# Two plain tiles instead of four at three feed-forward entries of a decoder trunk

## The chip, the core and the metric

The kernel runs on one core of a Trainium2 chip. The metric is device time in microseconds (us) of one execution. Five engines of the core matter here: TensorE (PE in the profile; its weight loads are PEld), VectorE (DVE), ScalarE (ACT), GpSimd (POOL) and SyncE (SP). SP and POOL are here mostly queues that issue transfers (DMAs). Each engine works through its own instructions in order, and waits on semaphores for the others.

## What is computed

The reference is a decoder trunk of two layers on 512 tokens with 1024 features, all in float32. Each layer is

```
x = x + 0.5 * swiglu(rms_norm(x, ffn1_norm[l]), ffn1_w_in[l], ffn1_w_out[l])
h = rms_norm(x, mix_norm[l]) @ w_mix_in[l]
...                                   # three token mixers on h give y
x = x + y @ w_mix_out[l]
x = x + 0.5 * swiglu(rms_norm(x, ffn2_norm[l]), ffn2_w_in[l], ffn2_w_out[l])
```

with `rms_norm(x, g) = x * rsqrt(mean(x*x) + 1e-6) * g` and `swiglu(h, w_in, w_out) = (silu(gate) * up) @ w_out`, where `gate` and `up` are the two halves of `h @ w_in`. A feed-forward block (FFN) has 2816 hidden features, 22 tiles of 128. There are four FFNs: two in each layer.

## The kernel before

**Layout.** The residual stream lies transposed in `xT`: 8 tiles of 128 features by 512 tokens. A float32 product is made from three matmuls on parts: a high part (rounded to the type that TensorE reads at full rate) and a low part (the remainder) of each operand, and high*high, high*low, low*high are summed (`mm3`, lines 328, 336 and 337). So every weight block is first parted: ScalarE casts the high part (line 314 for plain work, line 810 for the other kind), VectorE subtracts it from the weights for the low part (lines 315 and 812). The two parts lie in a tile `hl`, of which there are three in turn.

**Two ways for the first FFN product.** A pair of hidden tiles (256 gate and 256 up features) can be made *plain*: for each of the 8 feature tiles of x, 4 output banks times 3 matmuls of 512 tokens, 96 matmuls. The plain way takes x times the norm's gain, without the factor 1/rms; the factor `inv` is multiplied onto the result afterwards (`clear`, `values`). Or it can be made in *halves*: a scheme with 7 products, P1 to P7 in the order `ORDER_IN` = P1, P2, P6, P5, P7, P3, P4, in place of 8 (Strassen's, in Winograd's form). Each product is 8 blocks times 3 matmuls of 256 tokens, 24 in all. The halves way needs sums of quarters of the *normalised* x (`xn`, parted into `xc`), and sums of quarters of the weights (`raw`, `sums`), so it can't begin before the norm's factor is known.

**An entry.** Where an FFN begins, the norm's factor isn't known yet: x has just been finished. So the first tiles are made plain, and meanwhile the squares are summed (`sqa`), averaged over the features by two matmuls with a matrix of 1/1024 (line 447), and turned into `inv`: on ScalarE Ln, Exp and Square (line 277) and a load of the table for Silu (line 268), on VectorE three steps (lines 431 to 433). `covered` is the number of plain tiles: 6 in the first FFN of the kernel (`cover`), and 4 in the other three (`enter`, lines 583 to 699). Those three are the second FFN of layer 0, the first FFN of layer 1 and the second FFN of layer 1. In the profile their plain work begins at 578.11, 902.70 and 1467.33 us. `enter` writes out by hand the order of the entry on ScalarE and VectorE: `follow` chains each instruction behind the one before it on its engine. After `inv`, VectorE makes the quarters of normalised x, `xn`, each by four operations of 256 tokens (line 619); ScalarE casts their sums to high parts (line 632), VectorE makes the low parts (635 and 637) and the sums (642).

**The planner.** `plan(covered)` lists the products of the halves way in order, and at which step each load, sum and part of weights is issued. The weight parts of a product are made three products ahead (`prepare`, lines 800 to 812). For the first halved pair, `halved` loads four weight quarters (line 863), adds one quarter onto another by a transfer that accumulates (line 786, on POOL), and `enter` prepares the weights of the first products itself. A second accumulating transfer (line 827) adds a tile from on-chip memory onto another.

**Before the entry.** The last four feature tiles of x are finished by a loop on VectorE: in the mixer's end the add of line 1230, in an FFN's end the scaled add of line 502. After each, `norm_part` makes x times gain as high and low part (lines 408 and 409) and the square and its sum (lines 424 and 425).

Of the kernel before, what the change touches and what calls it, by code (L numbers as in the profile page):

```python
# [24 lines left out]
P = 128  # L25
T = 512
# [14 lines left out]
FIRST = 6  # L41
# [118 lines left out]
class Trunk:  # L160
# [255 lines left out]

    def squared(self, j, xj, pool):
# [25 lines left out]

    def end_norm(self, bank, pool, parts, keep=False):
        nc = self.nc
        for n, part in enumerate(parts):
            nc.tensor.matmul(bank, self.ones_mean, part, start=n == 0, stop=n == 1)
# [10 lines left out]
    def ffn(self, w_in, w_out, next_gain, covered, begin=None, out=None):  # L458
        nc = self.nc
        tc = self.tc  # L460
        with tc.tile_pool(name=self.n("ffn"), bufs=1) as fp:
# [26 lines left out]
            for dg in range(2):  # L488
# [10 lines left out]
                for i in range(4):  # L499
                    j = dg * 4 + i  # L500
                    xj = self.xT[:, j, :]
                    nc.vector.scalar_tensor_tensor(
                        out=xj, in0=banks[i], scalar=0.5, in1=xj,
                        op0=ALU.mult, op1=ALU.add,
                    )
                    if next_gain is not None:
                        self.norm_part(j, fp)
# [75 lines left out]
    def enter(self, fp, w_in, then):  # L583
        nc = self.nc
        H = T // 2
        A, V = (lambda i, e=e: self.follow(e, i) for e in "av")

        def stream(f, banks, given):
            def parts(k, kk):
                r = slice(k * P, (k + kk) * P)  # L590
                return [w_in[r, f * P : (f + 2) * P], w_in[r, FF + f * P : FF + (f + 2) * P]]

            return self.stream_steps(
                [(bk, slice(c, c + P), None) for bk, c in zip(banks, (0, 256, 128, 384))],
                parts, self.xact, KD, given=given,
            )

        ba = self.next4()
        first = stream(0, ba, lambda k: k == KD - 2)
        for _ in range(4):  # L600
            next(first)
        parts = self.parted_norm(fp, ("g1", "g1"), 2, True)
        nb = self.bank("pt" if self.ntog % 2 == 0 else "po")
        bb = self.next4()
        second = stream(2, bb, lambda k: True)
        self.ngain = self.const.tile([P, KD], F32, tag="ngain", name=self.n("ngain"))
        A(nc.scalar.activation(self.ngain, self.gain, AF.Copy, scale=-1.0))
        next(second)
        self.end_norm(nb, fp, parts, True)
        self.table(SILU)  # L610
        next(first, None)
        next(then)
        X, self.xc, lows = {}, {}, {}

        def quarter(a, b):
            X[a, b] = t = fp.tile([P, 4, H], F32, tag=f"r{2 + 2 * a + b}", name=self.n("xn"))
            for k in range(4):
                i = 4 * a + k
                V(nc.vector.scalar_tensor_tensor(
                    out=t[:, k, :], in0=self.xT[:, i, b * H : (b + 1) * H],  # L620
                    scalar=(self.gain if a == b else self.ngain)[:, i : i + 1],
                    in1=self.inv[:, b * H : (b + 1) * H], op0=ALU.mult, op1=ALU.mult,
                ))

# [19 lines left out]
        def both(name):  # L644
            high(name)
            lows[name]()

        def row():
            next(second)
            next(second, None)  # L650

        cleared = {}

        def clear(f, i):
            banks = bb if f else ba
            cleared[f, i] = self.clear(fp, banks[2 * i], banks[2 * i + 1], True)

        def values(f, i):
            self.values(fp, f, i, *cleared.pop((f, i)), True)

# [4 lines left out]
        next(second)  # L665
        next(second)
        high("P2")
        quarter(0, 1)
# [1254 lines left out]
```

## Time and profile before

| | us |
|---|---|
| median of 3 runs | 1802.08 (1801.78 to 1804.31) |
| the profiled execution | 1801.38 |
| its span, from first to last instruction | 1799.6 |
| TensorE busy | 1792.0 |
| VectorE busy | 1430.1 |
| ScalarE busy | 1001.0 |
| POOL busy | 176.6 |

The page gives busy times, the chain of work that ended last, and the costliest groups of instructions by line. A row such as `L810 ACT CAST hl<-w 128x1024 ... x322 | 336.8, 1050 | 305.9 ...` reads: line 810, on ScalarE, a cast that writes the tile `hl` from `w`, 322 times, 336.8 us in all, 1050 ns each, with 305.9 us of idle time ahead of them. A row of the timeline gives start, length, engine, line, operation, tiles and shape; `x4` says that four such instructions were merged into one row. Instructions of one engine overlap a little, so the distance between two starts is shorter than a length. TensorE's rows overlap strongly, and for it only the distance between starts is used.

### The profile page before, as it was taken

What the parts mean: (1) busy time and instruction counts of PE and PEld (TensorE: products, weight loads), DVE (VectorE), ACT (ScalarE), POOL (GpSimd) and SP (SyncE); (2) the same over time, 40 slices, a digit from 0 to 9 for tenths busy, and PEclk for the clock granted to TensorE, in tenths of its full rate; (3) what the DMA queues carried; (4) which work ended last, traced back from release to release, by engine and by line L of the source; (5) the groups of instructions that cost most, each with busy time, mean ns of one, the idle gap of its engine ahead of it and who ended that gap; (6) DMA issues with size and microseconds to landing.
All of it is one profiled execution on the core that took longest, in us unless ns stands there. A gap on an engine that the chain in (4) does not pass through costs nothing.

```text
span 1799.6 us, 34747 instructions
## 1 busy us (share of the span) xinstructions
PE 1792.0 (100%) x14271; PEld 1681.0 (93%) x14271; DVE 1430.1 (79%) x2006; ACT 1001.0 (56%) x1445; POOL 176.6 (10%) x184
## 2 busy tenths in 40 slices
PE   9999999999999999999999999999999999999999
PEld 7899999899888899999889999998998888999997
DVE  9889787676888798879679887876868879888793
ACT  5455554464776465556446555555547755555551
POOL 0011120100000002112001111201000000020210
PEclk9999999999999999999999999999999999999999
DMA  7659793233433857868265786913334346597762
GB/s 207 180 133 196 169 188 97 71 82 84 106 98 108 222 130 170 194 163 166 82 207 133 169 185 175 187 65 83 78 85 116 89 144 179 141 185 190 160 133 94
DMA packets 244638, 254.09 MB, mean 141 GB/s; under 512 B 18904, under 2 KB 228576, under 8 KB 244480
## 3 DMA queue, kind: packets, MB, share of 16 engines
q1 hardware_dynamic: 189424, 182.38, 33.7%
q0 software_dynamic: 54752, 69.23, 23.8%
q8 instruction: 112, 1.84, 0.4%
q14 instruction: 46, 0.38, 0.1%
q10 hardware_dynamic: 304, 0.27, 0.0%
HBM read 223.98 MB, written 2.10 MB: 126 GB/s over the span
## 4 chain that ended last, share of the span: by engine, by line
PE 94%; DVE 2%; ACT 2%; DMA 1%; issue 1%; SPq 0%; POOL 0%; ACTq 0%; DVEq 0%; POOLq 0%
PE mm L328 14%; PE mm L336 14%; PE mm L337 14%; PE sc L328 6%; PE sc L336 6%; PE sc L337 6%; PE pt L336 6%; PE pt L328 6%; PE pt L337 6%; PE po L328 4%; PE po L336 4%; PE po L337 4%; PE po L1654 1%; PE pt L1698 1%; PE pt L1352 1%
## 5 line engine op out<-in xcount | busy, mean ns | idle before, releaser
L810 ACT CAST hl<-w 128x1024 fp32r<-128x1024 f32 x322 | 336.8, 1050 | 305.9 <-PE mm L337 80.4
L812 DVE TENSOR_TENSOR hl<-w,hl 128x1024 fp32r<-128x1024 f32 x322 | 391.8, 1220 | 96.7 <-ACT hl L810 96.7
L315 DVE TENSOR_TENSOR hl<-st,hl 128x512 fp32r<-128x512 f32 (+3 forms) x196 | 162.5, 830 | 116.2 <-ACT hl L314 115.0
L314 ACT CAST hl<-st 128x512 fp32r<-128x512 f32 (+3 forms) x196 | 143.1, 732 | 174.3 <-PE po L337 66.8
L328 PE MATMUL mm<-xc,hl 128*128 128x256 f32 (+1 forms) x733 | 201.3, 276 | 0.0
L336 PE MATMUL mm<-xc,hl 128*128 128x256 f32 x728 | 201.2, 276 | 0.0
L337 PE MATMUL mm<-xc,hl 128*128 128x256 f32 x728 | 201.0, 276 | 0.0
L328 PE MATMUL sc<-xc,hl 128*128 128x256 f32 (+1 forms) x532 | 146.0, 276 | 0.0
L336 PE MATMUL sc<-xc,hl 128*128 128x256 f32 x528 | 146.0, 276 | 0.0
L337 PE MATMUL sc<-xc,hl 128*128 128x256 f32 x528 | 145.8, 276 | 0.0
L328 PEld LDWEIGHTS mm<-xc,hl 128*128 128x128 f32 x733 | 137.4, 188 | 0.2
L337 PEld LDWEIGHTS mm<-xc,hl 128*128 128x128 f32 x728 | 136.7, 188 | 0.0
L336 PEld LDWEIGHTS mm<-xc,hl 128*128 128x128 f32 x728 | 136.7, 188 | 0.0
L328 PE MATMUL pt<-xc,hl 128*128 128x256 f32 (+1 forms) x482 | 132.6, 276 | 0.0
L336 PE MATMUL pt<-xc,hl 128*128 128x256 f32 x480 | 132.6, 276 | 0.0
L337 PE MATMUL pt<-xc,hl 128*128 128x256 f32 x480 | 132.5, 276 | 0.0
L328 PE MATMUL mm<-x,hl 128*128 128x512 f32 x272 | 107.6, 396 | 0.0
L336 PE MATMUL mm<-x,hl 128*128 128x512 f32 x272 | 106.3, 391 | 0.0
L337 PE MATMUL mm<-x,hl 128*128 128x512 f32 x272 | 106.2, 390 | 0.0
L328 PEld LDWEIGHTS sc<-xc,hl 128*128 128x128 f32 x532 | 99.7, 188 | 0.2
L336 PEld LDWEIGHTS sc<-xc,hl 128*128 128x128 f32 x528 | 99.1, 188 | 0.0
L337 PEld LDWEIGHTS sc<-xc,hl 128*128 128x128 f32 x528 | 99.1, 188 | 0.0
(517 smaller groups left out, 5575.0 us busy)
## 6 DMA issues: line engine op xcount, KB each, us to landing
w<-in_ffn_w_in_dram SPq DMA_DIRECT2D x140, 512.0 KB, 5.1
w<-in_ffn_w_out_dram SPq DMA_DIRECT2D x64, 512.0 KB, 5.2
w<-in_ffn_w_out_dram POOLq DMA_DIRECT2D x56, 512.0 KB, 7.2
st<-in_w_mix_in_dram SPq DMA_DIRECT2D x88, 256.0 KB, 2.8
st<-in_ffn_w_in_dram SPq DMA_DIRECT2D x70, 256.0 KB, 3.1
w<-in_ffn_w_in_dram POOLq DMA_DIRECT2D x35, 512.0 KB, 8.9
w<-S POOLq DMA_DIRECT2D x35, 512.0 KB, 4.7
st<-in_ffn_w_out_dram SPq DMA_DIRECT2D x24, 512.0 KB, 5.3
```

What stands on the lines that cost most here:

```text
L314: a = nc.scalar.copy(hi, src[:, c : c + w])
L315: b = nc.vector.tensor_sub(lo, src[:, c : c + w], hi)
L328: i = nc.tensor.matmul(acc[:, c], ah, bh[:, c], start=first and c.start == 0, stop=False, skip_group_check=True,)
L336: nc.tensor.matmul(acc, a, b, start=False, stop=False, skip_group_check=True)
L337: i = nc.tensor.matmul(acc, c, d, start=False, stop=last, skip_group_check=True)
L810: A(nc.scalar.copy(hi, src))
L812: return lambda: V(nc.vector.tensor_sub(lo, src, hi))
L1352: nc.tensor.matmul(bank[hh][rows[par], at + x * n : at + (x + 1) * n], held[rows[hh], c * CH : (c + 1) * CH], moving(rows[hh], c), start=T ...
L1654: nc.tensor.matmul(self.ob[:, t0 + u * P : t0 + 2 * P], V[:, j, h % 4].rearrange("p a d -> p (a d)"), part[:, j, u:, :].rearrange("p i t - ...
L1698: nc.tensor.transpose(tb[:, j * P : (j + 1) * P], p[:, j * P : (j + 1) * P], self.ident)
```

## The change

At the three entries two tiles are made plain, not four; the second pair goes the halves way. The work around it is written out anew:

- In the loops that finish the last four x tiles ahead of a changed entry, the squares and their sums come first, right behind each add (`norm_late`). The parts of x times gain for these four tiles (`scaled`) move into the entry, two tiles at a time.
- The averaging matmuls (`mean`) are issued apart from the rest of the norm (`factor`).
- The quarters of normalised x are made in two steps: ScalarE scales x by the gain (`grown`, before `inv` is needed), and VectorE multiplies a whole quarter by `inv` in one operation.
- For the first two products, P1 and P2, the low part of the weights is made in another way (`prepare` with `carried`): ScalarE writes the negated high part into the low tile, and a transfer on POOL adds the weights onto it. The high part is cast after that. In the kernel before, VectorE subtracts.
- The plain pair's results are cleared and multiplied out later, at steps 8 to 12 of the halves way.

The diff, cut to its core:

```
-FIRST = 6
+FIRST, COVERED = 6, 2
...
+    def norm_late(self, js, pool, update):
+        V = lambda i: self.follow("v", i)
+        for j in (*js, None):
+            if j is not None:
+                V(update(j))
+            if j != js[0]:
+                V(self.nc.vector.tensor_add(self.sqacc, self.sqacc, sq))
+            if j is not None:
+                sq = pool.tile([P, T], F32, tag=self.tt, name=self.n("sq"), bufs=self.tb)
+                self.follow("a", self.nc.scalar.activation(sq, self.xT[:, j, :], AF.Square))
...
+                if dg and entered:
+                    self.norm_late(range(4, 8), fp, update)
+                    return
...
-        def quarter(a, b):
+        def grown(a, b):
             X[a, b] = t = fp.tile([P, 4, H], F32, tag=f"r{2 + 2 * a + b}", name=self.n("xn"))
             for k in range(4):
                 i = 4 * a + k
-                V(nc.vector.scalar_tensor_tensor(
-                    out=t[:, k, :], in0=self.xT[:, i, b * H : (b + 1) * H],
-                    scalar=(self.gain if a == b else self.ngain)[:, i : i + 1],
-                    in1=self.inv[:, b * H : (b + 1) * H], op0=ALU.mult, op1=ALU.mult,
-                ))
+                A(nc.scalar.activation(
+                    t[:, k, :], self.xT[:, i, b * H : (b + 1) * H], AF.Copy,
+                    scale=(self.gain if a == b else self.ngain)[:, i : i + 1],
+                ))
+
+        def quarter(a, b):
+            V(nc.vector.tensor_mul(
+                X[a, b], X[a, b], self.inv[:, b * H : (b + 1) * H].unsqueeze(1).to_broadcast([P, 4, H])
+            ))
...
+        next(plain)
+        norm = self.parted_norm(fp, ("g1", "g1"), 2, True)
+        self.mean(nb, norm)
+        self.ngain = self.const.tile([P, KD], F32, tag="ngain", name=self.n("ngain"))
+        A(nc.scalar.activation(self.ngain, self.gain, AF.Copy, scale=-1.0))
+        next(plain)
+        next(then)
+        next(plain)
+        for j in (4, 5):
+            self.scaled(j, self.xT[:, j, :], True)
+        next(plain)
+        next(plain)
+        self.factor(nb, fp, True)
+        self.table(SILU)
+        grown(0, 0)
+        for j in (6, 7):
+            self.scaled(j, self.xT[:, j, :], True)
+        next(plain)
+        grown(1, 0)
         quarter(0, 0)
         high("P1")
         quarter(1, 0)
         lows["P1"]()
-        next(second)
-        next(second)
+        grown(0, 1)
         high("P2")
+        self.given["carried"](0)
         quarter(0, 1)
         lows["P2"]()
-        quarter(1, 1)
-        next(second)
-        next(second)
+        grown(1, 1)
         add((0, 0), (0, 1))
         high("P5")
-        clear(0, 0)
+        quarter(1, 1)
         lows["P5"]()
-        next(second)
-        next(second)
-        next(second, None)
         add((0, 0), (1, 1))
         high("P6")
+        self.given["carried"](1)
         self.given["total"]()
         lows["P6"]()
-        self.given["prepare"](0)
-        self.given["prepare"](1)
-        clear(0, 1)
-        add((0, 1), (1, 1))
         next(then)
...
+            if carried:
+                A(nc.scalar.activation(lo, src, AF.Copy, scale=-1.0))
+                G(nc.gpsimd.dma_start(lo.bitcast(F32), src, accum_op=ALU.add))
             A(nc.scalar.copy(hi, src))
...
-            ffn1_w_in[l], ffn1_w_out[l], mix_norm[l], 4 if l else FIRST,
+            ffn1_w_in[l], ffn1_w_out[l], mix_norm[l], COVERED if l else FIRST,
```

As the engines' queues stand after the change, the order at the first of the three entries is this. On VectorE, ahead of the entry, from the add of tile 4 (bank `mm_6728`) on; `hl` from `st` is the low part of plain weights, `x_...` the low part of x times gain, `sqa` the sum of squares. Before, twelve rows:

```order
L1230 TENSOR_TENSOR xT<-mm_6728,xT 128x512
L1230 TENSOR_TENSOR xT<-mm_6729,xT 128x512
L1230 TENSOR_TENSOR xT<-mm_6730,xT 128x512
L315 TENSOR_TENSOR hl_6881<-st_6878,hl_6881 128x1024
L425 TENSOR_TENSOR sqa_6705<-sqa_6705,sq_6781 128x512
L409 SCALAR_TENSOR_TENSOR x_963_6784<-xT,gain_5444,x_963_6784 128x512
L425 TENSOR_TENSOR sqa_6705<-sqa_6705,sq_6788 128x512
L409 SCALAR_TENSOR_TENSOR x_965_6791<-xT,gain_5444,x_965_6791 128x512
L425 TENSOR_TENSOR sqa_6705<-sqa_6705,sq_6795 128x512
L409 SCALAR_TENSOR_TENSOR x_967_6798<-xT,gain_5444,x_967_6798 128x512
L1230 TENSOR_TENSOR xT<-po_6731,xT 128x512
L315 TENSOR_TENSOR hl_6911<-st_6908,hl_6911 128x1024
```

And after the change:

```order
L1245 TENSOR_TENSOR xT<-mm_6728,xT 128x512
L1245 TENSOR_TENSOR xT<-mm_6729,xT 128x512
L423 TENSOR_TENSOR sqa_6705<-sqa_6705,sq_6781 128x512
L1245 TENSOR_TENSOR xT<-mm_6730,xT 128x512
L423 TENSOR_TENSOR sqa_6705<-sqa_6705,sq_6785 128x512
L1245 TENSOR_TENSOR xT<-po_6731,xT 128x512
L423 TENSOR_TENSOR sqa_6705<-sqa_6705,sq_6789 128x512
L423 TENSOR_TENSOR sqa_6705<-sqa_6705,sq_6793 128x512
L449 TENSOR_TENSOR sh_6838<-sqa_6705,sh_6837 128x512
L315 TENSOR_TENSOR hl_6887<-st_6884,hl_6887 128x1024
```

The two weight remainders and the four low parts of x no longer stand between the adds and the sum's last step.

On ScalarE, from the table load of the norm on; `xn` are the quarters, `xc` the high parts of the products' x operands, `hl` from `w` the parts of halved weights. Before:

```order
L268 ACT_TABLE_LOAD
L632 ACTIVATE xc_6981<-xn_6976 128x1024
L314 CAST hl_7017<-st_7014 128x1024
L632 CAST xc_7020<-xn_6984 128x1024
L314 CAST hl_7061<-st_7058 128x1024
L632 CAST xc_7065<-xn_6976 128x1024
L277 ACTIVATE gi_7068<-gi_7068 128x512
L314 CAST hl_7101<-st_7098 128x1024
L632 CAST xc_7129<-xn_6976 128x1024
L810 CAST hl_7135<-w_6969 128x1024
L810 CAST hl_7138<-w_6973 128x1024
```

After:

```order
L626 ACTIVATE xn_6971<-xT,ngain_6843 128x256 x4
L643 ACTIVATE xc_6977<-xn_6936 128x1024
L626 ACTIVATE xn_6982<-xT,ngain_6843 128x256 x4
L643 CAST xc_6987<-xn_6971 128x1024
L823 ACTIVATE hl_6990<-w_6877 128x1024
L825 CAST hl_6990<-w_6877 128x1024
L626 ACTIVATE xn_6996<-xT,gain_5444 128x256 x4
L643 CAST xc_7002<-xn_6936 128x1024
L643 CAST xc_7008<-xn_6936 128x1024
L823 ACTIVATE hl_7011<-w_6881 128x1024
L825 CAST hl_7011<-w_6881 128x1024
L825 CAST hl_7021<-S_7015 128x1024
```

The negated copy for P2's weights (L823 on `hl_7011`) stands behind four more scalings and the high parts for P5 (`xc_7002`) and P6 (`xc_7008`). On TensorE the first halved product now follows the last plain matmul like this, and its fourth row is the one that waits for a transfer issued by POOL (DMASW):

```order
L337 MATMUL pt_6805<-x_994_6944,hl_6923 128x512
L328 MATMUL mm_7024<-xc_6977,hl_6990 128x128 [waits Activation_49]
L328 MATMUL mm_7024<-xc_6977,hl_6990 128x128
L336 MATMUL mm_7024<-xc_6978,hl_6990 128x256 [waits DVE_49]
L337 MATMUL mm_7024<-xc_6977,hl_6990 128x256 [waits DMASW3_49]
```

In the kernel before, the row in that place (`hl_7135`) waits for VectorE.

106 lines of the change are left out of this document (45 added, 61 removed).

## The prediction

> **What bounds the kernel now.** I read the page first, then the waits of TensorE, then the timeline around the first changed entry, then the groups and the table of transfers. From the page, the span, the busy times and the chain that ended last:
>
> ```profile
> span 1799.6 us, 34747 instructions
> PE 1792.0 (100%) x14271; PEld 1681.0 (93%) x14271; DVE 1430.1 (79%) x2006; ACT 1001.0 (56%) x1445; POOL 176.6 (10%) x184
> PE 94%; DVE 2%; ACT 2%; DMA 1%; issue 1%; SPq 0%; POOL 0%; ACTq 0%; DVEq 0%; POOLq 0%
> ```
>
> TensorE is the bound, and the table of its waits (out, releaser, total us, count, longest) has six rows, of 3.6 us together; the two largest and the smallest:
>
> ```profile
> PE pt L1698 <- DVE QA L1600: 1.3, 2, 0.6
> PE mm L1815 <- DVE z L1802: 1.2, 1, 1.2
> ...
> PE po L447 <- ACT sh L438: 0.2, 1, 0.2
> ```
>
> None belongs to a product of a changed entry, so every matmul removed there is worth its full time, and every wait added there costs its full time. TensorE at the first entry (start, length), and the two other starts of plain work:
>
> ```profile
> 578.11 0.39 PE L328 MATMUL sc<-x,hl 128*128 128x512 f32 x1
> 622.12 0.33 PE L328 MATMUL sc<-xc,hl 128*128 128x128 f32 x2
> 623.16 0.28 PE L337 MATMUL sc<-xc,hl 128*128 128x256 f32 x1
> 626.00 0.28 PE L328 MATMUL sc<-xc,hl 128*128 128x256 f32 x1
> 902.70 0.39 PE L328 MATMUL mm<-x,hl 128*128 128x512 f32 x1
> 1467.33 0.39 PE L328 MATMUL sc<-x,hl 128*128 128x512 f32 x1
> ```
>
> From 578.11 to 622.12 stand 4 x 48 matmuls of plain work and 2 for the mean, 0.2269 us each. From 623.16 to 626.00 stand 25 steps of 256 columns, 0.1136 each.
>
> **What the change removes.** A pair of tiles goes from 96 x 0.2269 = 21.78 to 168 x 0.1136 = 19.08 us of TensorE: 2.7 an entry, 8.1 in three. The queues show the exchange: 72 matmuls more at each entry.
>
> **What it takes away with them: cover.** Plain work lasted 44.0 us, and now lasts 98 x 0.2269 = 22.2, to 600.35. By then the norm and the first operands must stand, so I lay out the new order with the durations of before. Rows of VectorE near the three starts, and of the norm:
>
> ```profile
> 576.68 1.23 DVE L315 TENSOR_TENSOR hl<-st,hl 128x1024 fp32r<-128x1024 f32 x1
> 577.82 1.88 DVE L1230 TENSOR_TENSOR xT<-mm,xT 128x512 f32<-128x512 f32 x3
> 595.10 0.69 ACT L277 ACTIVATE nr<-po,epsc 128x512 f32<-128x512 f32 x1 [4.86 <-PE po L447]
> 595.82 0.63 ACT L277 ACTIVATE nr<-nr 128x512 f32<-128x512 f32 x1
> 596.49 0.63 ACT L277 ACTIVATE nt<-nr 128x512 f32<-128x512 f32 x1
> 597.14 1.28 ACT L268 ACT_TABLE_LOAD   x1
> 597.15 0.69 DVE L431 SCALAR_TENSOR_TENSOR nt<-po,nt 128x512 f32<-128x512 f32 x1 [5.65 <-ACT nt L277]
> 597.88 0.43 DVE L432 TENSOR_SCALAR nt<-nt 128x512 f32<-128x512 f32 x1
> 598.34 0.69 DVE L433 TENSOR_TENSOR inv<-nr,nt 128x512 f32<-128x512 f32 x1
> 599.06 1.67 DVE L619 SCALAR_TENSOR_TENSOR xn<-xT,gain,inv 128x256 f32<-128x256 f32 x4
> 602.24 1.21 DVE L635 SCALAR_TENSOR_TENSOR xc<-xn,xc 128x1024 fp32r<-128x1024 f32 x1
> 898.54 1.22 DVE L315 TENSOR_TENSOR hl<-st,hl 128x1024 fp32r<-128x1024 f32 x1 [4.21 <-ACT hl L314]
> 1467.05 1.88 DVE L1230 TENSOR_TENSOR xT<-mm,xT 128x512 f32<-128x512 f32 x3
> ```
>
> The sizes of ScalarE's and VectorE's steps (timeline rows first, then groups, where the second number behind the bar is the mean ns of one):
>
> ```profile
> 580.93 1.32 ACT L408 ACTIVATE x<-xT,gain 128x512 fp32r<-128x512 f32 x2
> 617.11 1.99 ACT L810 CAST hl<-w 128x1024 fp32r<-128x1024 f32 x2
> L810 ACT CAST hl<-w 128x1024 fp32r<-128x1024 f32 x322 | 336.8, 1050 | 305.9 <-PE mm L337 80.4
> L812 DVE TENSOR_TENSOR hl<-w,hl 128x1024 fp32r<-128x1024 f32 x322 | 391.8, 1220 | 96.7 <-ACT hl L810 96.7
> L408 ACT ACTIVATE x<-xT,gain 128x512 fp32r<-128x512 f32 x40 | 28.3, 713 | 14.3 <-DVE xT L502 11.6 <-DVE xT L1230 2.7
> L1572 ACT ACTIVATE V<-mm,invc 128x256 fp32r<-128x256 f32 x12 | 5.7, 473 | 6.8 <-PE mm L337 3.9 <-DVE V L1573 3.0
> ```
>
> Two casts take 1.99, so a second costs 0.94; two 512-wide scalings take 1.32, a second 0.62. Three VectorE adds take 1.88, so a step is 0.60. The new scaling of 256 columns has no row: 0.40, which is L1572's 0.47 less an overlap like these. The product of a whole quarter with `inv` has none either: 1.21, like L635, which also reads two sources of 1024 columns; its upper bound is 1.67, the four L619 operations that it replaces.
>
> *Up to `inv`.* VectorE is free for the adds at 577.82. Eight steps (four adds, three sums, the last sum) end at 583.06; ScalarE parts the result to 583.72, VectorE to 584.44, and after the two matmuls the mean stands at 585.1, where TensorE loses at most 0.2. On ScalarE Ln is queued behind the negated gain, two casts of plain weights and two scalings (x tiles 4 and 5), so it begins at 586.97; Square ends at 589.02; beside the table load VectorE takes its three steps (1.9 us), and `inv` stands at 590.93, 8.1 earlier than in the rows above (599.03).
>
> *The first remainder.* ScalarE scales a quarter and x tiles 6 and 7, then a second quarter, to 594.9. VectorE, after the low parts of those two tiles, has the first quarter times `inv` at 595.25. ScalarE: high part for P1 to 596.34, four scalings to 597.86, high part for P2 to 598.81, negated copy to 599.86. Only then can the transfer start. Transfers that accumulate from on-chip memory, with the median landing, its spread over the same 35, and the group beside it that accumulates from HBM:
>
> ```profile
> w<-S POOLq DMA_DIRECT2D x35, 512.0 KB, 4.7
> DMA to landing us min/median/max: 4.5/4.7/6.4
> w<-in_ffn_w_in_dram POOLq DMA_DIRECT2D x35, 512.0 KB, 8.9
> ```
>
> The new ones have the size, queue and two on-chip ends of the first group, so I take 4.7, and 0.1 for the issue: landed at 604.7. TensorE reaches P1's third matmul, which needs this remainder, at 600.35 + 0.23 = 600.6 and waits 4.1. The whole matmul queue stands behind it; the cast of P1's high weights, at 600.7 itself a little late, disappears in this wait. P1 ends at 607.2.
>
> *The second remainder.* ScalarE goes on from 600.7: four scalings to 602.3, high part for P5 to 603.4. Then it must wait: P6's high part needs the last quarter (VectorE 602.45 to 603.67), behind it in VectorE's queue P5's low part (to 604.81), then the sum (to 605.95). P6's high part ends at 607.04, and the second negated copy, queued behind it although raw weights are all it needs, at 607.99. It lands at 612.8. TensorE would be at P2's third matmul at 607.4 and waits 5.4.
>
> *Afterwards* I find each operand ahead of its product; the closest is P3's, needed at 623.6 and ready at 622.7. So an entry loses 4.1 + 5.4 = 9.5. This sum is simply the second landing less the time at which an unhindered TensorE would ask for it (600.35 + 26 x 0.1136 = 603.3): the first transfer's length divides it differently, and leaves it as it is.
>
> *The other entries.* At 1467.05 VectorE stands against the start (1467.33) as at the first entry: 9.5. At the second, the low part of 898.54 and one more, 1.14 each by the distance of the two first VectorE rows above, leave it free at 900.82, 1.9 ahead of 902.70 in place of 0.3: 1.6 less, 7.9.
>
> **Sum**: 9.5 + 7.9 + 9.5 = 26.9 of waits less 8.1 = +18.8. The profiled execution took 1801.38 (its span and 1.8 around it), so 1820.2; the median of the runs shown is 0.7 above it, so **1821**.
>
> The VectorE subtractions that the transfers replace (two of 1.22 an entry) buy nothing here: VectorE isn't what the copies wait for, except ahead of P6's high part.
>
> **Bounds.** Transfers of 4.5 to 6.4: -0.6 to +5.1 in three entries. Scaling of 256 columns between half of the 512-wide step (0.31) and L1572's full 0.47, eight to twelve of them on the chain in an entry: about -3 to +3. Quarter times `inv` at 1.67: +0.5 each on up to three in the chain, +4. From -3.6 to +12 if all fell together; I take 1813 to 1830, a little wider below, since a compressed step may uncover a second one.
>
> The Trainium skill ("DMA: Bandwidth & Descriptors", section on the anatomy of one DMA on the SWDGE path) gives about 2.0 us fixed and 436 GB/s, from which 512 KB are an estimate of 3.2 us. By it the time would be some 4.5 lower, 1816.5. The trace's 35 landings, none under 4.5, decide against it.
>
> **Rivals.**
>
> *The cover suffices.* Without added waits the time would be 1802.1 - 8.1 = 1794. For it: `inv` comes 8.1 us earlier, and the two preparations depend on no norm. Against it: they are queued behind scalings and high parts that do. Even at half of the wait found, 4.7 an entry, it would be 1802.1 + 14 - 8 = 1808. To be faster, the second remainder must land by 603.3 + 2.7 = 606.0, 6.8 ahead of where I have it, more than the bounds allow. 0.05, with 0.02 for a sum that ends near nothing.
>
> *The clock drops in the waits.* TensorE's first rows of the execution:
>
> ```profile
> 3.78 1.12 PE L1766 MATMUL mm<-ident,xs 128*128 128x128 f32 x4
> 6.71 0.60 PE L1766 MATMUL mm<-ident,xs 128*128 128x128 f32 x4
> ```
>
> The same four matmuls take 1.12 us early and 0.60 later, so the array begins at half rate. If a wait of 4 to 5 us brings that back, P1's and P2's matmuls run at 0.227: for the 22 after each wait +2.5, of which the first is absorbed by the wait for the second landing. +2.5 an entry, 7.5 in all: about 1828.5. Before has no idle TensorE above 1.2 us, so nothing in it decides. 0.13. The Trainium skill ("TensorE: Matmul & The Clock Gate", Part 1 on the HAM clock gate) has the half clock return after an idle window of about 3.4 us, for one busy window; the start rows agree, no run shows it inside a kernel.
>
> *The transfers queue behind POOL's others.* Loads that accumulate from HBM on the same queue land in 8.9. If the new ones share their fate, the second lands 4.2 later: +12.6, 1834. Against it: the on-chip group stands at 4.7 in the same pattern of products. 0.08.
>
> **How the numbers follow.** Forecast 0.72 (waits at both remainders, 1813 to 1830), clock 0.13, queue 0.08, cover 0.05, none 0.02. The range of the forecast takes in the clock's case; what it leaves out is part of the queue's and the cover's. A measurement of this kernel tells 0.2% from no change, 3.6 us: faster 0.05, same 0.02, slower 0.93.
>
> **What would show it.** In the profile after, TensorE's waits on transfers into `hl` in products P1 and P2, three each: near 4.1 and 5.4 (2.5 and 5.4 at the second entry). `inv` some 8 us earlier; the second L823 row some 30 us behind the start of plain work; POOL's new transfers at 4.5 to 6.4. The clock's case shows as 256-column steps of 0.227 behind a wait and a granted clock under 1.00. Wrong I'd be if ScalarE reached the second copy before VectorE's sum, if short scalings cost far under 0.3, or if a wait fell at a product that I have as ready.

## The result: 2.2% slower, twice the predicted loss

The changed kernel takes 1842.58 us (median of 4 runs, 1841.35 to 1844.66); the kernel before, measured beside it, 1802.28. The ratio is 1.0223, with a 95% interval of 1.0205 to 1.0240. Slower was predicted, but 1821 with a range up to 1830: the loss is 40 us and not 19.

The page of the changed kernel, its span, busy times and chain:

```profile
span 1840.7 us, 35231 instructions
PE 1799.9 (98%) x14487; PEld 1695.8 (92%) x14487; DVE 1438.5 (78%) x1970; ACT 1040.0 (56%) x1517; POOL 188.5 (10%) x196
PE 85%; DVE 5%; ACT 4%; DMA 3%; issue 2%; SPq 0%; ACTq 0%; POOL 0%; DVEq 0%; POOLq 0%
```

TensorE has 216 matmuls more, shorter ones: the change does what it says. But its busy time is 8 us longer where 8.1 less was due, so some matmuls ran slowly, and 40.8 us of the span are idle (7.6 before). TensorE's waits (out, then the instruction or transfer that ended the wait, total us, count, longest):

```profile
PE mm L337 <- DMA hl<-w: 23.4, 6, 6.8
PE po L328 <- DVE hq L722: 2.7, 3, 0.9
PE mm L328 <- ACT u L946: 2.3, 2, 1.4
PE sc L1549 <- ACT flh L1543: 1.6, 1, 1.6
PE po L328 <- ACT g L943: 1.3, 3, 0.5
```

The first row is the predicted one: six waits on the two new transfers, `L337` being the third matmul of a product. Its 23.4 us stand against 26.9 predicted; that the two are so near is luck, as the part on the prediction tells. The rows under it were not predicted, and slow running only as a rival. The first entry on TensorE, from the first plain matmul to the first matmul of the FFN's second product (which reads `m`):

```profile
578.24 0.39 PE L328 MATMUL sc<-x,hl 128*128 128x512 f32 x1
...
601.25 0.44 PE L328 MATMUL mm<-xc,hl 128*128 128x128 f32 x2 [0.40 <-ACT hl L825]
601.52 0.33 PE L336 MATMUL mm<-xc,hl 128*128 128x256 f32 x1
608.63 0.58 PE L337 MATMUL mm<-xc,hl 128*128 128x256 f32 x1 [6.78 <-DMA hl<-w]
609.00 0.42 PE L328 MATMUL mm<-xc,hl 128*128 128x256 f32 x1
...
613.06 0.35 PE L336 MATMUL mm<-xc,hl 128*128 128x256 f32 x1
...
615.45 0.39 PE L337 MATMUL mm<-xc,hl 128*128 128x256 f32 x1 [1.69 <-DMA hl<-w]
...
684.51 0.28 PE L328 MATMUL pt<-m,hl 128*128 128x256 f32 x1
```

The kernel before reached the same place here:

```profile
671.22 0.28 PE L328 MATMUL mm<-m,hl 128*128 128x256 f32 x1
```

This stretch is the measure used below. Before, it is 671.22 - 578.11 = 93.11 us, at all three entries; with the 2.69 us of saved matmuls it would be 90.42. After, it is 106.27 at the first entry, and by the same rows of the others (916.14 to 1020.56, 1495.11 to 1601.27) 104.42 and 106.16: they *lose* 15.9, 14.0 and 15.7 us, 45.6 together. Less the 8.1 saved, that is 37.5 of the 41.1 us by which the span grew. The other 3.6 lie outside the entries, 3.0 of them between the second and the third; 1.6 of it is the wait at L1549 above.

Both transfers took longer than the 4.7 us that the prediction used. Their issues on POOL (start, length of the issue), and their landings (us, all six):

```profile
600.57 0.89 POOL L824 DMA_DIRECT2D hl<-w  x1 [11.39 <-ACT hl L823]
608.78 0.85 POOL L824 DMA_DIRECT2D hl<-w  x1 [7.33 <-ACT hl L823]
```

```profile
DMA to landing us min/median/max: 6.3/7.3/8.1
```

On ScalarE the order was as laid out: the second negated copy (second L823 row) stands behind the high part for P6, which waits for VectorE's sum.

```profile
599.21 1.05 ACT L823 ACTIVATE hl<-w 128x1024 fp32r<-128x1024 f32 x1
...
606.49 1.04 ACT L643 CAST xc<-xn 128x1024 fp32r<-128x1024 f32 x1 [2.75 <-DVE xn L653]
607.44 1.05 ACT L823 ACTIVATE hl<-w 128x1024 fp32r<-128x1024 f32 x1
```

It ends at 608.49, 30.3 us behind the start of plain work; the prediction had 29.9.

### The profile page after: what moved, and what is told of

It is laid out like the page before. It is cut to its first block, busy times and chain, and to the rows that moved or that the text cites. A ratio compares the mean times of both kernels' runs of the same rounds, so it can differ in the third digit from the quotient of the medians.

```text
span 1840.7 us, 35231 instructions
## 1 busy us (share of the span) xinstructions
PE 1799.9 (98%) x14487; PEld 1695.8 (92%) x14487; DVE 1438.5 (78%) x1970; ACT 1040.0 (56%) x1517; POOL 188.5 (10%) x196
## 4 chain that ended last, share of the span: by engine, by line
PE 85%; DVE 5%; ACT 4%; DMA 3%; issue 2%; SPq 0%; ACTq 0%; POOL 0%; DVEq 0%; POOLq 0%
PE mm L328 15%; PE mm L337 15%; PE mm L336 15%; PE po L328 4%; PE po L336 4%; PE po L337 4%; PE sc L328 4%; PE pt L328 4%; PE pt L337 4%; PE pt L336 4%; PE sc L337 4%; PE sc L336 4%; DMA st<-in_w_mix_in_dram 1%; PE po L1671 1%; DMA hl<-w 1%
## 5 line engine op out<-in xcount | busy, mean ns | idle before, releaser
L825 ACT CAST hl<-w 128x1024 fp32r<-128x1024 f32 x340 | 355.8, 1049 | 341.2 <-PE mm L337 123.3
L337 PE MATMUL mm<-xc,hl 128*128 128x256 f32 x1584 | 442.9, 280 | 23.4 <-DMA hl<-w 23.4
L328 PE MATMUL mm<-xc,hl 128*128 128x256 f32 (+1 forms) x1595 | 443.1, 279 | 3.3 <-ACT u L946 2.3
L336 PE MATMUL mm<-xc,hl 128*128 128x256 f32 x1584 | 442.5, 279 | 0.0
L337 PEld LDWEIGHTS mm<-xc,hl 128*128 128x128 f32 x1584 | 301.4, 190 | 24.7 <-DMA hl<-w 24.7
L328 PEld LDWEIGHTS mm<-xc,hl 128*128 128x128 f32 x1595 | 302.7, 190 | 4.9 <-ACT u L946 2.7
L336 PEld LDWEIGHTS mm<-xc,hl 128*128 128x128 f32 x1584 | 301.4, 190 | 0.0
L315 DVE TENSOR_TENSOR hl<-st,hl 128x512 fp32r<-128x512 f32 (+2 forms) x184 | 148.1, 806 | 111.2 <-ACT hl L314 110.1
L314 ACT CAST hl<-st 128x512 fp32r<-128x512 f32 (+2 forms) x184 | 130.5, 712 | 164.6 <-PE mm L337 50.0
L328 PE MATMUL po<-xc,hl 128*128 128x256 f32 x545 | 151.1, 278 | 4.0 <-DVE hq L722 2.7
L336 PE MATMUL po<-xc,hl 128*128 128x256 f32 x544 | 150.6, 277 | 0.0
L337 PE MATMUL po<-xc,hl 128*128 128x256 f32 x544 | 150.5, 277 | 0.0
L328 PE MATMUL pt<-m,hl 128*128 128x256 f32 x448 | 123.9, 276 | 0.0
L337 PE MATMUL pt<-m,hl 128*128 128x256 f32 x448 | 123.8, 276 | 0.0
L336 PE MATMUL pt<-m,hl 128*128 128x256 f32 x448 | 123.8, 276 | 0.0
L328 PE MATMUL sc<-m,hl 128*128 128x256 f32 x448 | 123.8, 276 | 0.0
L337 PE MATMUL sc<-m,hl 128*128 128x256 f32 x448 | 123.8, 276 | 0.0
L336 PE MATMUL sc<-m,hl 128*128 128x256 f32 x448 | 123.8, 276 | 0.0
L328 PEld LDWEIGHTS po<-xc,hl 128*128 128x128 f32 x545 | 102.3, 188 | 5.1 <-issue 3.2
L336 PEld LDWEIGHTS po<-xc,hl 128*128 128x128 f32 x544 | 102.3, 188 | 0.0
L337 PEld LDWEIGHTS po<-xc,hl 128*128 128x128 f32 x544 | 102.2, 188 | 0.0
```

The source lines that it names most:

```text
L314: a = nc.scalar.copy(hi, src[:, c : c + w])
L315: b = nc.vector.tensor_sub(lo, src[:, c : c + w], hi)
L328: i = nc.tensor.matmul(acc[:, c], ah, bh[:, c], start=first and c.start == 0, stop=False, skip_group_check=True,)
L336: nc.tensor.matmul(acc, a, b, start=False, stop=False, skip_group_check=True)
L337: i = nc.tensor.matmul(acc, c, d, start=False, stop=last, skip_group_check=True)
L825: A(nc.scalar.copy(hi, src))
```

## The experiments

The theory carried into them (A): the second landing sets most of the loss, it is late by its place in ScalarE's order, and it is late again because the loads of later weights fill the DMA engines. Rivals: the half clock costs it (B), the accumulation is slow by itself (C), VectorE has no time left (D). All runs in one table; "loss" is the mean over the three entries of the stretch above less 90.42.

| kernel | median us | ratio to before (95%) | loss per entry, us |
|---|---|---|---|
| the change | 1842.58 | 1.0223 (1.0205 to 1.0240) | 15.2 |
| without the transfers | 1834.30 | 1.0171 (1.0156 to 1.0187) | 12.1 |
| later loads held back | 1844.09 | 1.0225 (1.0210 to 1.0240) | 15.5 |
| TensorE kept busy | 1843.72 | 1.0229 (1.0212 to 1.0246) | 15.6 |
| transfers early | 1837.21 | 1.0189 (1.0174 to 1.0204) | 13.0 |
| VectorE subtracts | 1831.81 | 1.0163 (1.0148 to 1.0178) | 12.1 |
| new order | 1825.77 | 1.0130 (1.0114 to 1.0145) | 9.7 |
| new order, VectorE subtracts | 1828.84 | 1.0148 (1.0131 to 1.0165) | 11.0 |
| new order, less VectorE work | 1820.84 | 1.0107 (1.0090 to 1.0124) | 7.8 |
| new order, P3 and P4 later | 1822.91 | 1.0121 (1.0106 to 1.0136) | 8.5 |
| plain results later | 1838.97 | 1.0196 (1.0181 to 1.0211) | 13.6 |
| all of it | 1821.14 | 1.0099 (1.0083 to 1.0116) | 7.8 |

### What the transfers cost

```
             if carried:
                 A(nc.scalar.activation(lo, src, AF.Copy, scale=-1.0))
-                G(nc.gpsimd.dma_start(lo.bitcast(F32), src, accum_op=ALU.add))
             A(nc.scalar.copy(hi, src))
```

> The changed kernel without the two accumulating transfers of each entry: the low part of P1's and P2's weights is then only the negated copy, so these two products of the three pairs lack their remainder (the output is not the reference's), and every other instruction stays. Theory A (the second transfer's landing sets the entry's loss): P2 then waits for ScalarE's cast that follows the second negated copy, 31 us after the start of plain work in place of the landing at 37 us. 6 us less in each entry: 1824 to 1830 us. Theory B (the half clock after the waits costs the larger part): the wait ahead of P2 is then still 5 to 6 us long, the clock falls in it and nothing behind absorbs it, so at most 4 us an entry come back: 1830 to 1837. If the transfers were hidden behind something else that ends equally late, 1840 to 1843.

1834.3: only 3 us an entry come back, theory A's number is missed and B's range is met. The wait ahead of P2 at the first entry, and the granted clock around it. (A row by stretches gives the bounds, the length, the busy time and count of PE, PEld, DVE, ACT and POOL, then the granted clock, the busy share of the DMA engines and their GB/s; the clock is the third value from the end.)

```profile
609.02 0.58 PE L328 MATMUL mm<-xc,hl 128*128 128x256 f32 x1 [5.12 <-ACT hl L824]
```

```profile
604.00:609.00 5.00, 0.00 (x0) 0.00 (x0) 4.30 (x4) 2.97 (x4) 0.00 (x0) 0.99 1.01 308
609.00:613.00 4.00, 3.98 (x21) 3.98 (x22) 3.05 (x3) 2.36 (x3) 2.21 (x2) 0.59 0.66 120
```

As expected P2 goes 6 us earlier, when ScalarE's cast behind the copy is done. But P2 then runs at a clock of 0.59, and the later waits stay. So the transfers are a smaller part than theory A had it: even without them P2 waits 5 us for the place of its weights in ScalarE's order.

### Why they took 7 us

```
             raw[u, q] = t = self.res.tile([P, 4, 2 * P], F32, tag=f"x{tag}", name=self.n("w"))
+            if held:
+                held.pop()
+                A(nc.scalar.copy(t[:, 0, :1], self.gain[:, :1]))
             S(nc.sync.dma_start(t, src(u, q)))
```

> The changed kernel, in which the weight loads for the second halved pair (eight of 512 KB on SP's queue) can't begin before the second negated copy has run: ScalarE writes one column of the first load's target right behind it. Theory A (the loads of later weights fill the sixteen DMA engines, and this lengthens the new transfers from 4.7 to 6.3-8.1 us): the first transfer lands in 4.5 to 5.5, the second too or nearly, so the second landing stands near 35 us behind the start of plain work in place of 37. The loads themselves come some 20 us later, so a new wait on them may follow; the time, 1834 to 1860, is not the verdict, the landings are. Rival C (an accumulation onto a tile, or VectorE's work on it, is slow by itself): the new transfers stay at 6.3 to 8.1 us.

The landings of the six transfers, and the DMA engines at the first entry (the last two values of a row: busy share, GB/s), in this kernel:

```profile
DMA to landing us min/median/max: 4.5/5.3/6.0
```

```profile
600.00:606.00 6.00, 2.29 (x12) 1.51 (x11) 5.02 (x6) 4.27 (x7) 0.89 (x1) 1.00 0.46 87
606.00:610.00 4.00, 4.00 (x22) 3.87 (x20) 3.32 (x3) 2.98 (x5) 0.68 (x1) 0.57 0.00 0
```

and in the changed kernel:

```profile
600.00:606.00 6.00, 1.45 (x7) 0.79 (x5) 5.02 (x5) 3.73 (x7) 0.89 (x1) 1.00 1.10 343
606.00:610.00 4.00, 1.37 (x6) 1.37 (x7) 2.79 (x3) 3.52 (x4) 0.85 (x1) 0.55 1.04 300
```

With the loads out of the way the share of the DMA engines falls from 1.10 and 1.04 to 0.46 and 0.00, and the transfers from 7.3 to 5.3 us in the median; the shortest, 4.5, is as short as the shortest of the on-chip group before. Rival C falls. The second transfer is not freed wholly: it is issued at 609.32, and from 610 to 616 the held loads bring the share back to 0.91. The time stays, as the second landing hardly moved (615.3). The Trainium skill says it of transfers from ScalarE, SyncE and GpSimd ("DMA: Bandwidth & Descriptors", section "Issuing engines are not separate DMA queues"): whichever engine issues them, they run on the same 16 DMA engines and interleave. The two pairs of rows agree.

### The half clock

```
         next(plain)
+        for _ in range(13):
+            self.mean(nb, norm)
         grown(1, 0)
```

> The changed kernel with 26 idle matmuls (the averaging product repeated, 512 columns each, 5.9 us) behind the last plain matmul, ahead of P1, at the three entries; their result is read by nobody. They lie inside the wait for the first transfer. Theory A: the second landing sets the end, so what P1 wins by a full clock (21 matmuls of 0.214 in place of 0.114, 2.1 us) is lost in a longer wait ahead of P2: 1840 to 1848, the upper half if the longer second wait lets the clock fall in P2. Theory B (the clock costs): 2 us less in each entry, 1834 to 1837.

1843.72 is 1.1 us above the change, too little to tell the two apart, and in theory A's range. The two waits at the first entry, and the granted clock behind the second:

```profile
609.23 0.39 PE L337 MATMUL mm<-xc,hl 128*128 128x256 f32 x1 [1.68 <-DMA hl<-w]
616.33 0.58 PE L337 MATMUL mm<-xc,hl 128*128 128x256 f32 x1 [4.00 <-DMA hl<-w]
```

```profile
613.00:619.00 6.00, 2.67 (x12) 2.67 (x13) 4.62 (x4) 1.77 (x3) 1.94 (x2) 0.62 0.34 65
```

P1 now runs at full speed, and TensorE reaches P2's third matmul early and waits 4.0 us there where it waited 1.7; then P2 runs at half rate. So the half clock behind the *first* wait cost nothing, because the second landing stood behind it. Behind the *second* wait it costs up to 2 us, unless a later wait takes it up: the later waits at L946 of the changed kernel, 0.9 us at the first entry and 1.4 at the third, are absent here, and the loss is nearly the same. The run without transfers, too, had P2 at half rate.

### The place in ScalarE's order

```
         next(plain)
+        self.given["carried"](0)
         grown(1, 0)
         quarter(0, 0)
         high("P1")
+        self.given["carried"](1)
         quarter(1, 0)
...
         high("P2")
-        self.given["carried"](0)
...
         high("P6")
-        self.given["carried"](1)
```

> The changed kernel with the two negated copies, their transfers and the casts behind them placed earlier in ScalarE's order: the first ahead of the second quarter's scalings, the second right behind the high part of P1's x. Nothing else changes. Theory A: the transfers start 594.6 and 599.1 in place of 600.6 and 608.8 (first entry), the second lands near 606, TensorE waits 2 us for the first and little for the second; then P6 comes late, since its x parts stand behind the last quarter on VectorE (ready about 612, wanted at 606), so 6 of the 12 us that the entry loses by the second landing come back: 1822 to 1828. If what follows is as late as the second landing was, 1838 to 1843.

1837.21: 2 us an entry, not 6. The waits of TensorE:

```profile
PE mm L328 <- ACT g L934: 7.0, 3, 2.6
PE mm L337 <- DMA hl<-w: 6.0, 4, 2.3
PE mm L328 <- ACT g L916: 4.7, 3, 2.6
PE mm L328 <- ACT u L946: 2.7, 2, 1.4
```

The waits on the transfers fall from 23.4 to 6.0 us, so the place was indeed what made them late (the transfers by themselves are no shorter here, 7.6 to 8.5 us). But 14 us stand in other rows. A bank is the place on the chip into which the matmuls of a product add. P6, P7 and P3 wait, by the rows, for ScalarE's copies of the banks that they write to (L934, L916, L946), and these copies are queued behind casts that wait for VectorE. The expectation had P6 as late as it came, and nothing behind it.

```
         high("P2")
-        self.given["carried"](0)
+        low = self.given["prepare"](0)
         quarter(0, 1)
         lows["P2"]()
+        low()
...
         high("P6")
-        self.given["carried"](1)
+        low = self.given["prepare"](1)
         self.given["total"]()
         lows["P6"]()
+        low()
```

> The changed kernel with one part undone: the low parts of P1's and P2's weights are subtracted by VectorE (behind the low part of P2's x, and behind the low part of P6's x) in place of negated copy and transfer; all other work keeps its place. Theory A (the transfers are late and slow; VectorE, ready 1.2 us after the cast, is earlier): P1's remainder stands some 24 us behind the start of plain work in place of 30, P2's some 32 in place of 37. P6's and P5's weight parts come 1.2 us later on VectorE. By the laid-out order the first pair loses 7 us where it lost 12: 4 to 5 us less in each entry, 1826 to 1833 us. Theory D (VectorE is the engine that has no time left, which the transfers relieve): what TensorE no longer waits for the transfers, it waits for VectorE: 1838 to 1846.

1831.81, in theory A's range: undoing the transfers alone gives back 11 of the 40 us. Rival D falls *for this order*: VectorE had gaps. VectorE's busy time in 20 us is the third busy value, first for the changed kernel, then for the order that comes next:

```profile
591.00:611.00 20.00, 12.82 (x58) 10.61 (x57) 15.22 (x15) 16.15 (x27) 1.74 (x2) 0.88 1.10 314
```

```profile
591.00:611.00 20.00, 17.79 (x111) 15.76 (x110) 19.43 (x27) 12.66 (x17) 3.90 (x4) 1.00 1.10 298
```

### A new order

`whole` is the quarter as it was made before the change, four operations on VectorE.

```
         self.table(SILU)
-        grown(0, 0)
+        cast = self.given["carried"](0)
+        whole(0, 0)
         for j in (6, 7):
...
-        grown(1, 0)
-        quarter(0, 0)
+        cast()
         high("P1")
-        quarter(1, 0)
+        whole(1, 0)
         lows["P1"]()
         grown(0, 1)
-        high("P2")
-        self.given["carried"](0)
         quarter(0, 1)
-        lows["P2"]()
-        grown(1, 1)
+        high("P2")
+        cast = self.given["carried"](1)
+        cast()
         add((0, 0), (0, 1))
+        self.given["total"]()
+        lows["P2"]()
         high("P5")
-        quarter(1, 1)
         lows["P5"]()
+        whole(1, 1)
         add((0, 0), (1, 1))
+        low = self.given["prepare"](2)
+        low()
         high("P6")
-        self.given["carried"](1)
-        self.given["total"]()
         lows["P6"]()
```

> The changed kernel with the entry's order written anew around what depends on nothing: the first negated copy as soon as the norm's steps on ScalarE are done, the second behind P2's x; VectorE makes three of the four quarters whole, by four operations each, as before the change (it is free when the factor stands), ScalarE scales one alone; the parts of P6's weights ahead of P6's x. Theory A (the order on ScalarE is what makes the operands late): laid out, the first pair loses 3.7 us in an entry where it lost 12.2; with what the runs so far had beyond the laid-out loss (3 to 5 us: half clock behind a wait, waits in the second pair), 1814 to 1828 us. It stays above the kernel before, since 2.7 us are saved in an entry. Theory E (the two tiles give enough cover if the order is right): under 1802. If the order doesn't matter and the engines' sum of work does: 1835 to 1843.

1825.77: 17 of the 40 us were the order, and which engine makes the quarters. The second of the two rows above shows what it cost: VectorE, at 15.2 of 20 us before, is now at 19.4, full. TensorE's clock is 1.00 there, and no wait is longer than 2.2 us:

```profile
PE mm L337 <- DMA hl<-w: 6.6, 5, 2.2
PE mm L328 <- ACT g L931: 5.2, 3, 2.2
PE mm L328 <- ACT u L961: 4.2, 3, 1.4
```

The same order with subtractions differs from it by two places, `low = self.given["prepare"](i)` and `low()` for `carried` and `cast`:

> Much the same new order with VectorE's subtractions in place of the two transfers: two operations more on VectorE in an entry, one fewer per product on ScalarE. Laid out, the first pair loses 5.4 us in an entry (P6's x, behind two more VectorE operations, is the latest) against 3.7 with the transfers: 1818 to 1832 us, 3 to 6 us above the kernel with the transfers in that order. Rival: the transfers, at 7 to 8 us each among the loads, cost as much there as the subtractions: the two within 2 us.

1828.84, 3.1 us above the order with transfers. That is by the expected amount, but the intervals of the two ratios overlap: that the transfers help once VectorE is full is likely, and not settled.

```
-            self.xc[name] = hi, lo
+            left = name in ("P1", "P2", "P5", "P6")
+            self.xc[name] = hi, hi if left else lo
...
             def low():
+                if left:
+                    return
```

> The kernel with the new order, with less for VectorE to do: it leaves out the low parts of the x operands of P1, P2, P5 and P6 at the three entries (four operations of 1.2 us; their high part is taken twice, so these products of the first pair are wrong). Theory A2 (in the new order VectorE, without a gap from 591 to 611 at the first entry, sets when P7 and P3 can go): the waits ahead of P7 and P3, 3.6 us in an entry, go, and those for the two transfers, 2.2, stay: 1814 to 1820 us. Rival F (the chain of hand-overs between ScalarE and VectorE sets it, not VectorE's work): within 2 us of the new order's 1825.8.

1820.84, against 1825.77 with that work: 5 us, more than F's 2, and 0.8 above the range that A2 expected. By the waits (three lines lower in this kernel), P7's row, 5.2 us at L931, is down to 0.4, and P3's, 4.2 at L961, to 3.4:

```profile
PE mm L337 <- DMA hl<-w: 7.2, 5, 2.4
PE mm L328 <- ACT u L964: 3.4, 3, 1.4
...
PE mm L328 <- ACT g L934: 0.4, 1, 0.4
```

VectorE's work sets P7's wait; P3's has another cause.

### The small waits behind

```
-            1: lambda: (high("P3"), lows["P3"](), add((0, 0), (1, 0))),
-            2: lambda: (high("P4"), lows["P4"]()),
+            2: lambda: (high("P3"), lows["P3"](), add((0, 0), (1, 0))),
+            3: lambda: (high("P4"), lows["P4"]()),
```

> The kernel with the new order, with the x parts of P3 and P4 put one product later in the order of ScalarE and VectorE, so that ScalarE's copies of the finished banks (which P7 and P3 need before they write there) stand ahead of casts that wait for VectorE. Theory G (these copies, queued behind such casts, are what TensorE waits for ahead of P7 and P3): 1 to 2 us less in an entry: 1820 to 1823 us. If P7's and P3's operands are as late themselves: within 1.5 us of 1825.8.

1822.91, in the expected range, with an interval that overlaps the one of the new order. The trace supports it: the waits on L931 and L961, 9.4 us together in the new order, have become these two, one of 0.9, and 0.7 that are left at L961:

```profile
PE mm L328 <- ACT g L931: 2.4, 2, 1.4
...
PE mm L328 <- ACT hl L839: 2.4, 2, 1.2
```

Then the plain pair's results, in the changed kernel:

```
-            8: lambda: clear(0),
-            9: lambda: values(0),
-            11: lambda: clear(1),
-            12: lambda: values(1),
+            10: lambda: clear(0),
+            11: lambda: values(0),
+            14: lambda: clear(1),
+            15: lambda: values(1),
```

> The changed kernel with the plain pair's results cleared and multiplied out at the steps 10, 11, 14 and 15 of the halves way, not 8, 9, 11 and 12; nothing else is changed. Theory H (these operations, ahead of the reads of the bank that TensorE writes next, make the two waits 44 and 56 us behind the first halved product, 0.5 and 1.1 us in each entry): both waits go, 1836 to 1840 us, and no more than that. If they only move to other banks: 1841 to 1844.

1838.97: theory H. The two rows on `po` (2.7 and 1.3 us in the changed kernel) are gone from the table of waits, and nothing took their place.

The last kernel is the new order with both of these edits:

> The new order, with the x parts of P3 and P4 one product later and the plain pair's results at the steps 10, 11, 14 and 15: all that the runs so far point to, the attempt at a version that beats both. By the parts (1822.9 with the first two, up to 4.7 less by the third): 1818 to 1823 us, still above the kernel before, since an entry saves 2.7 us of matmuls and loses 6 to 7. If a good order is enough for two tiles: under 1804.

1821.14, as expected: half of the loss is gone, and it is still 1.0% slower than the kernel before. No version with two plain tiles beats it here. Moving the plain results brought 3.6 us in the changed kernel, and only 1.8 in this order, where the intervals with and without it overlap.

## Why the prediction was half right

**What held.** The bound; the exchange of 72 matmuls an entry (what it saves was not measured by itself); `inv` at 591.3 (predicted 590.9); ScalarE's and VectorE's order with every step in it, to 0.5 us over 30; the two waits at the places named, each three times. Scaling 256 columns and the product with `inv` cost what was taken for them: four scalings are 1.69, one product 1.22.

**What was luck.** The waits on the transfers, 23.4 us against 26.9, come near in the sum and not in the parts: an entry was to wait 4.1 (at the second entry 2.5) and then 5.4 us, and it waited 5.2 to 6.8 and then 1.0 to 2.0. The landings were later than predicted, which lengthens the waits, and behind the first wait P1 ran at half rate, 0.21 us a step, which fills some 2 us of the second.

**What failed, term by term.** The sum was +18.8 us, the span grew by 41.1.

1. *"I take 4.7" for the transfers.* They took 6.3 to 8.1. With the 0.4 us by which the copy came later, the second landing stands at 37.2 us behind the start where 34.7 were predicted, at the first entry; over three entries (at the others that matmul starts at 950.75, 34.6 behind 916.14, and at 1531.97, 36.9 behind 1495.11) 6.2 us more. The median came from 35 transfers in all phases of the FFN; the maximum of 6.4 that was quoted beside it was the nearer row. The run with held loads shows why: the entry is where the loads of the next pair run, and the DMA engines move 300 GB/s and over.
2. *"Afterwards I find each operand ahead of its product".* This step failed most: 12.5 us over three entries come behind the second landing. The operands were listed, but not the *banks*: P3 may write only when ScalarE has copied P5's result (L946), and that copy is queued behind a cast that waits for VectorE, as these rows of the first entry show; the second pair waits for reads of `po` (L722) and for a copy (L943) behind the plain pair's results. The waits of the second pair, 4 us over the three entries, are shown by the run that moves the plain results; the other waits at banks are read from the traces, and supported by the two runs that touch them. With L946 these waits are 6.3 of the 12.5 us. The half clock behind the second wait at the second entry is some 1.9, the slow rhythm described at the end 2.1, and about 2 are not assigned.

```profile
625.16 1.06 ACT L643 ACTIVATE xc<-xn 128x1024 fp32r<-128x1024 f32 x1 [1.00 <-DVE xn L653]
627.06 0.59 ACT L946 ACTIVATE u<-mm 128x512 f32<-128x512 f32 x1
627.70 0.38 PE L328 MATMUL mm<-xc,hl 128*128 128x256 f32 x1 [0.91 <-ACT u L946]
```

3. *Outside the entries* 3.6 us were lost, and none was predicted. Between the second and the third entry TensorE's waits grew from 0.6 to 3.1 us, 1.6 of them at L1549 and 0.9 at L1648; why they did wasn't tried.

**The rivals.** The clock's case had the right fact and the wrong account: it put 2.5 us an entry on P2 behind the second landing, while the waits there, 1.0 to 2.0 us, were mostly too short. The queue's case came nearest in size to the transfers (8.9 there, 7.3 in fact), for another reason: not POOL's queue, which issued nothing else from 589 to 615 us at the first entry, but the DMA engines that all queues share. The sentence that VectorE's subtractions "buy nothing here" was true, and too weak: they would have been 11 us *better* than the transfers.

**The range** treated the bounds of each term as all there is, and ended at 1830, below the 1833 that its own bounds (+12) lead to. The longer transfers alone would have stayed in it, at 1827. What broke it was a step costed at nothing.

## What to carry to other kernels

When cover is taken from a bound engine, list for each step behind it not only the operands but the buffers that it writes to, and who must read them first: an in-order queue that waits for one late operand holds back the copies that free banks for the next products. Price a transfer by the rows of the same stretch, with the share of the DMA engines there, not by a median over the kernel. And an order written for much cover is not an order for little: 21 of 40 us came back by order and by giving work back to VectorE here. The rest is only in part explained. VectorE is full for 20 us of an entry in the new order, and taking four of its operations out of each entry brought 5 us. In the last kernel the three entries still lose 23.3 us; 14.2 of them are waits of TensorE, and 4.7 are the slow rhythm described below.

## What the chip did that was not expected

**Half rate behind short waits.** Behind the wait of 6.8 us the matmuls start every 0.21 us from 609.00 to 613.06 and every 0.11 after. At the second entry, behind a *second* wait of 1.97 us, it came again. The second entry's second wait and the stretch behind it, granted clock third from the end:

```profile
948.80:950.70 1.90, 0.00 (x0) 0.00 (x0) 0.99 (x1) 1.37 (x2) 0.00 (x0) 1.00 0.09 17
951.00:954.40 3.40, 3.40 (x18) 3.40 (x18) 2.28 (x3) 1.06 (x1) 2.19 (x2) 0.52 0.53 96
```

That wait began about 1 us behind the end of the previous slow stretch. But a slow stretch just before isn't needed: at the third entry of the kernel with early transfers the first wait of all, 1.86 us behind plain work without a wait, was followed by half rate.

```profile
1517.21 0.39 PE L337 MATMUL mm<-xc,hl 128*128 128x256 f32 x1 [1.86 <-DMA hl<-w]
```

```profile
1518.00:1521.40 3.40, 3.40 (x18) 3.40 (x17) 3.40 (x4) 1.34 (x2) 0.00 (x0) 0.50 1.05 257
```

In the new order, on the other hand, waits up to 2.2 us left the clock at 1.00, and in the same order with subtractions one of 2.6 us did. The length of a wait alone doesn't decide it; what does stays open. The Trainium skill ("TensorE: Matmul & The Clock Gate", Part 1 on the HAM clock gate) puts the drop behind an idle window of about 3.4 us, and the return behind a busy one of the same length; the windows run free of the kernel. The 4.1 us of slow matmuls at 609 and the 3.4 us of the two later stretches agree; 1.97 and 1.86 us of idle time are less than such a window, and the clock fell all the same.

**Two rhythms at full clock.** Matmuls of 256 columns start every 0.1133 us, or every 0.1178, for hundreds in a row, at a granted clock of 1.00 in both. The ends of one long stretch of each in the changed kernel:

```profile
657.88 0.28 PE L337 MATMUL po<-xc,hl 128*128 128x256 f32 x1
...
698.11 0.33 PE L328 MATMUL mm<-xc,hl 128*128 128x128 f32 x2
```

```profile
992.41 0.28 PE L336 MATMUL po<-xc,hl 128*128 128x256 f32 x1
...
1034.69 0.34 PE L328 MATMUL mm<-xc,hl 128*128 128x128 f32 x2
```

355 steps in 40.23 us, and 359 in 42.28. In the first entry the rhythm changes behind the waits at 615.45 (to the slow one) and 645.13 (back), and not behind those at 627.70 and 657.21; the slow stretch above begins behind a wait of 0.91 us and ends at a matmul that is issued in two halves. In the kernel before, without waits, the steps of the same pairs at the first entry are nearly all of the faster kind. 234 slow steps at the first entry cost 1.1 us. In the last kernel, at a granted clock of 1.00, the three entries have 1076 slow steps, 4.7 us, so this is no longer a small part of what is lost there; what sets the rhythm wasn't tried.
